# A transformer trunk on one core: the first 512 query channels projected together, row by row

## The chip, the cores and the metric

The kernel runs on 1 core of one Trainium2 chip. The time is that of the device for one execution, in microseconds (us); the runs of the kernel before have a median of 479.36 us (479.05 to 480.07, three runs). Lower is better. The core's engines are TensorE (PE in the profile, with its weight loads as PEld), VectorE (DVE), ScalarE (ACT), GpSimd (POOL) and SyncE (SP), which here issues all loads and stores.

## The reference

One layer of a hybrid decoder: 256 positions, 1024 channels, float32.

```python
def mixer_sublayer(x, w_in, ...):
    qa, ka, va, qd, kd, vd, b_gate, c_gate, hc, gate_logits = jnp.split(x @ w_in, split_points, axis=-1)
    y_moba = moba_attention(heads(qa, 8), heads(ka, 8), heads(va, 8))
    y_conv = b_gate * causal_dwconv(c_gate * hc, w_short_conv)
    y_dil = dilated_mixture(heads(qd, 12), heads(kd, 12), heads(vd, 12))
    gates = jax.nn.sigmoid(gate_logits).reshape(b, s, 3, 1024)
    merged = gates[:, :, 0] * (y_moba @ w_moba_proj) + gates[:, :, 1] * (y_conv @ w_conv_proj) \
        + gates[:, :, 2] * (y_dil @ w_dil_proj)
    return merged @ w_mix_out

def conv_ffn_sublayer(x, w_up, w_ffn_conv, b_ffn_conv, w_down):
    u = causal_dwconv(x @ w_up, w_ffn_conv) + b_ffn_conv
    gate, val = jnp.split(u, 2, axis=-1)
    return (jax.nn.silu(gate) * val) @ w_down

x = layer_norm(DN_ALPHA * x + mixer_sublayer(x, ...), ln1_g, ln1_b)
x = layer_norm(DN_ALPHA * x + conv_ffn_sublayer(x, ...), ln2_g, ln2_b)
```

The change concerns the start alone: x is transposed, and the first columns of `x @ w_in` that are computed are those of the dilated attention, `qd` (768 channels), then `kd` (768) and `vd` (768).

## The kernel before

Products of float32 are made of three products of rounded halves: `split` rounds a tensor to a high part (a cast on ScalarE, line 149) and takes the rest as a low part (a difference on VectorE, line 150), and `mm3` (lines 200 to 202) multiplies high by high, low by high and high by low.

Weights come in blocks of 1 MB (1024 rows by 256 columns), in the order in which `block` and `columns` list them: three blocks of `qd`, three of `kd`, three of `vd`, and so on. `load_next` issues the load of the next block into one of three buffers `raw`, from SyncE's queue (line 124). A block has four pieces of 128 x 512; `prep` splits the next piece, and when the last piece of a block is split, its buffer is free and `load_next` issues another load into it. `ready` holds the split pieces, `used` counts those that are used up, and `prep` goes at most 10 pieces (`LEAD`) ahead of it. The first two blocks are loaded in four parts of 256 KB each, and between those of the first block the four parts of x (line 177).

`transpose_x` turns two of the eight slices of x (128 channels by 256 positions each) on TensorE into a bank of PSUM from the pool `att` (five banks), and splits them into `xTh` and `xTl`. `first_products` then multiplies with one piece of the first block: two slices of x, and two banks of 128 channels each (`o`, from the pool `acc`, which has three banks; the first was used by the warm-up). The other blocks go through `project`: for each half of 128 channels it takes one `acc` bank, multiplies through all eight slices (24 matmuls), and lets `tick` split further pieces and call `consume`, which copies the bank out. For queries and keys a bank is copied out in two halves of 64 partitions, by ScalarE and VectorE in turn (`queries`, lines 239 and 240).

`small_loads` issues five loads of some KB each (the weights of the two convolutions) behind the last block of queries, `rows` loads the two rows of the norm (512 KB each, since they are spread to all partitions), and `small_weights` turns the small loads on TensorE (lines 423 and 425), between the first and the second block of `kd`.

The order of the instructions on each engine is set by a scheduler when the program is built: it goes by the order of the code and takes later work ahead where it holds an engine to be free. On the chip each engine's instructions stand in that fixed order.

Of the kernel before, what the change touches and what calls it, by code (L numbers as in the profile page):

```python
# [14 lines left out]
P = 128  # L15
T = 256
D = 1024
KT = D // P
# [8 lines left out]
DIL_Q, DIL_K, DIL_V = 1536, 2304, 3072  # L27
# [3 lines left out]
RAW = 3  # L31
LEAD = 10
B2 = 61
WARM = 7


@with_exitstack
def trunk(ctx: ExitStack, tc, x, w_in, w_short_conv, w_moba_proj, w_dil_proj, w_conv_proj, w_mix_out,
          ln1_g, ln1_b, w_up, w_ffn_conv, b_ffn_conv, w_down, ln2_g, ln2_b, out):
    nc = tc.nc  # L40
# [12 lines left out]
    def fresh(name):  # L53
        serial[0] += 1
        return f"{name}{serial[0]}"

    def buf(dt=F32, shape=(P, 512)):
        return act.tile(list(shape), dt, tag="b2", name=fresh("b"), bufs=B2)

    def acc(shape=(P, 512)):  # L60
        return ps.tile(list(shape), F32, tag="acc", name=fresh("acc"), bufs=3)

    def att(shape=(P, 512)):
        return ps.tile(list(shape), F32, tag="att", name=fresh("att"), bufs=5)
# [5 lines left out]
    def block(*parts):  # L70

        blocks.append(parts)

    def kview(w, c0, c1, k0=0, k1=None):
        k1 = w.shape[0] // P if k1 is None else k1
        return w[k0 * P:k1 * P, c0:c1].rearrange("(k p) c -> p k c", p=P)

    def columns(base, n):
        for b in range(n):
            c = base + 256 * b  # L80
            block(kview(w_in, c, c + 256))

    columns(DIL_Q, 3)
    columns(DIL_K, 3)
    columns(DIL_V, 3)
    columns(MOBA_V, 2)
# [6 lines left out]
    for d in range(4):  # L93
        for g in range(3):
            columns(GATE + g * D + d * 256, 1)
        c = d * 256
# [11 lines left out]
    loads, pieces, ready = [], [], []  # L108
    used = [0]

    def load_next(between=None):
        i = len(loads)
        if i >= len(blocks):
            return
        r = act.tile([P, 2048], F32, tag="raw", name=fresh("raw"), bufs=RAW)
        at = 0
        for p in blocks[i]:
            k, c = p.shape[1:]
            step = 2 if i < 2 else k
            for k0 in range(0, k, step):  # L120
                if between:
                    between(k0 // step)
                n = step * c
                nc.sync.dma_start(r[:, at:at + n].rearrange("p (k c) -> p k c", c=c), p[:, k0:k0 + step, :])  # L124
                at += n
        loads.append(r)
        pieces.extend((r, c, c + 512 == at) for c in range(0, at, 512))

    def prep(n=1):

        for _ in range(n):
            i = len(ready)
            if i >= min(len(pieces), used[0] + LEAD):
                return
            r, c, last = pieces[i]
            h, l = buf(F32R), buf(F32R)
            split(r[:, c:c + 512], h, l)
            ready.append((h, l))
            if last:
                load_next()  # L140

    def take(n):

        i = used[0]
        assert len(ready) >= i + n, (len(ready), i, n)
        return ready[i:i + n]

    def split(src, h, l):
        nc.scalar.copy(h, src)  # L149
        nc.vector.tensor_sub(l, src, h.bitcast(F32))  # L150
# [4 lines left out]
    def tick(n, consume=None, ahead=1):  # L155


        used[0] += n
        while late:
            late.pop(0)()  # L160
        prep(n + ahead)
        if consume:
            consume()
        if side:
            side.pop(0)()
# [4 lines left out]
    wps = acc()  # L170
    for i in range(WARM):
        nc.tensor.matmul(wps, warm[:, :P], warm, start=True, stop=True)


    xs = act.tile([P, 2, D], F32, tag="xs", name="xs", bufs=2)
    xv = x.rearrange("(t p) c -> p t c", p=P)
    load_next(lambda c: nc.sync.dma_start(xs[:, :, c * 256:c * 256 + 256], xv[:, :, c * 256:c * 256 + 256]))  # L177
    for i in range(1, RAW):
        load_next()

    ident = const.tile([P, P], F32, name="ident")
    diff = const.tile([P, P], I32, name="diff")
# [3 lines left out]
    xTh = act.tile([P, KT, T], F32R, tag="xTh", name="xTh")  # L186
    xTl = act.tile([P, KT, T], F32R, tag="xTl", name="xTl")

    def transpose_x(k2):
        k = 2 * k2  # L190
        p = att((P, 2, T))
        for a in range(2):
            for t in range(2):
                nc.tensor.transpose(p[:, a, t * P:(t + 1) * P], xs[:, t, (k + a) * P:(k + a + 1) * P], ident)  # L194
        split(p, xTh[:, k:k + 2, :], xTl[:, k:k + 2, :])


    def mm3(o, ah, al, bh, bl, first, last):
# [10 lines left out]
    def project(consume, xh=xTh, xl=xTl, ahead=1):  # L209

        w = take(4)
        for c in range(2):
            o = acc((P, T))
            for k in range(KT):
                mm3(o, *cut(w, k, c * P, c * P + P), xh[:, k, :], xl[:, k, :], k == 0, k == KT - 1)
            tick(2, lambda: consume(c, o), ahead)
# [16 lines left out]
    def queries(store):  # L233

        def consume(c, o):
            q = buf(F32R, (P, 2, T))
            for a in range(2):
                s, n = HALF[a], HALF[1 - a]
                nc.scalar.copy(q[s, a, :], o[s, :])
                nc.vector.tensor_sub(q[n, a, :], o[s, :], q.bitcast(F32)[s, a, :])  # L240
            store.append(q)
        return consume
# [185 lines left out]


    dq, dk, dv = [[], [], []], [[], [], []], []  # L430
    o = [acc((P, T)) for _ in range(2)]

    def first_products(k2):
        w = ready[k2]
        for xt, i in ((xTh, 0), (xTl, 0), (xTh, 1)):
            for k in (2 * k2, 2 * k2 + 1):
                for c in range(2):
                    s = (k % 2) * 256 + c * P
                    nc.tensor.matmul(o[c], w[i][:, s:s + P], xt[:, k, :], start=k + i == 0 and xt is xTh,  # L439
                                     stop=k == KT - 1 and i == 1)  # L440

    for k2 in range(KT // 2):
        transpose_x(k2)
        prep()
        if k2:
            first_products(k2 - 1)
    first_products(KT // 2 - 1)
    q = queries(dq[0])
    for c in range(2):
        tick(2, lambda: q(c, o[c]), 1)  # L450
    for g in range(1, 3):
        project(queries(dq[g]), ahead=0)
    small_loads()
    gB, bB = rows(ln1_g, "gB"), rows(ln1_b, "bB")
# [5 lines left out]
    p, q = (dilated(c, dq, dk, dv, [t[:, c, :] for t in yd]) for c in range(2))  # L460
# [6 lines left out]
    for b in range(2):  # L467
# [21 lines left out]
        p, q = (moba(c, mq, mk, mv[b], [t[:, c, :] for t in ym]) for c in range(2))  # L489
# [15 lines left out]
    for d in range(4):  # L505
        gs = []
        for g in range(3):
            s = buf(F32, (P, 2, T))
# [5 lines left out]
        w = take(5)  # L514
        for c in range(2):
            for g, k0, n, ys in ((2, 0, 2, [yd]), (1, 2, 4, ycT), (0, 6, 4, ymT)):
                o = acc((P, T))
# [81 lines left out]
    w = take(4)  # L599
# [15 lines left out]
    def between():  # L615
        passed.append(prep(1))
        if len(passed) == 2:
            turn_x1(0, 0)
            turn_x1(0, 1)
# [29 lines left out]
    w = take(8)  # L649
    u = []  # L650
    for t in range(2):
        o = acc()
        s = slice(t * P, (t + 1) * P)
# [23 lines left out]
    for j in range(2, NJ, 2):  # L677
# [3 lines left out]
        while 2 < j < NJ - 2 and pend:  # L681
            w = take(4)
# [49 lines left out]
```

## Time and profile before

| | |
|---|---|
| profiled execution | 479.29 us |
| its span, from first to last instruction | 477.5 us |
| median of the runs | 479.36 us |
| TensorE busy | 466.5 us, 98% of the span |
| VectorE busy | 360.3 us, 75% |
| ScalarE busy | 271.0 us, 57% |
| mean granted clock of TensorE | 0.991 |
| bytes moved | 83.51 MB, mean 175 GB/s |

The span is what lies between the first and the last instruction; the rest of an execution's time lies around it. Matmuls are pipelined: the profile gives one as 283 ns, while they start 0.12 us apart. The idle time of an engine matters only where the chain of waits goes through it.

### The profile page before, as it was taken

To read this page: it belongs to the slowest core of one execution; us is meant where nothing else is said; L and a number is where in the kernel's file an instruction comes from. 1 tells how busy PE (TensorE), PEld (TensorE's weight loads), DVE (VectorE), ACT (ScalarE), POOL (GpSimd) and SP (SyncE) were. 2 spreads that over 40 slices of the span, in tenths; PEclk is the share of its full clock that TensorE was granted. 3 is DMA by queue.
4 is the path that set the end of the run, shared out by engine and by line. 5 is a ranking of instruction groups with operands and counts; after the bars stand their busy time and mean duration, and the time that the engine had idled before them with its cause. 6 is when DMAs were issued, how large, how long until landed. Compare 5 with 4: busy or idle time off the path is not lost.

```text
span 477.5 us, 9121 instructions
## 1 busy us (share of the span) xinstructions
PE 466.5 (98%) x3582; PEld 450.6 (94%) x3582; DVE 360.3 (75%) x775; ACT 271.0 (57%) x579; POOL 10.4 (2%) x29
## 2 busy tenths in 40 slices
PE   7999999999999999999999999999999999999993
PEld 4999999999999999999999899999999999999983
DVE  6788996778989757484748866997867676786966
ACT  4767774737668645454545316866555565564710
POOL 1100000010100000000000000000000000000000
PEclk8999999999999999999999999999999999999997
DMA  8986555254451745656465914657465545637002
GB/s 265 359 253 189 178 177 177 89 176 131 136 161 41 231 144 182 195 165 211 153 220 200 311 49 151 243 175 265 127 227 176 178 177 188 221 122 244 21 2 88
DMA packets 69502, 83.51 MB, mean 175 GB/s; under 512 B 1688, under 2 KB 64852, under 8 KB 69460
## 3 DMA queue, kind: packets, MB, share of 16 engines
q1 hardware_dynamic: 69460, 82.94, 53.3%
q8 instruction: 28, 0.46, 0.4%
q14 instruction: 14, 0.11, 0.1%
HBM read 81.89 MB, written 1.05 MB: 174 GB/s over the span
## 4 chain that ended last, share of the span: by engine, by line
PE 97%; DMA 1%; DVE 1%; SPq 0%; ACT 0%; issue 0%; DVEq 0%
PE acc L200 24%; PE acc L202 24%; PE acc L201 24%; PE att L201 7%; PE att L200 7%; PE att L202 7%; PE att L266 2%; PE acc L439 1%; PE att L287 1%; DMA xs<-in_x_dram 1%; PE att L194 0%; DVE r L551 0%; SPq L124 0%; SPq L177 0%; PE acc L594 0%
## 5 line engine op out<-in xcount | busy, mean ns | idle before, releaser
L150 DVE TENSOR_TENSOR b<-raw,b 128x512 fp32r<-128x512 f32 x300 | 196.1, 687 | 38.0 <-ACT b L149 35.6
L149 ACT CAST b<-raw 128x512 fp32r<-128x512 f32 x300 | 169.3, 620 | 6.2 <-DMA raw<-in_w_in_dram 2.9
L200 PE MATMUL acc<-xTh,b 128*128 128x256 f32 x432 | 122.9, 284 | 0.0
L201 PE MATMUL acc<-xTl,b 128*128 128x256 f32 x432 | 122.2, 283 | 0.0
L202 PE MATMUL acc<-xTh,b 128*128 128x256 f32 x432 | 122.2, 283 | 0.0
L200 PE MATMUL acc<-x1Th,b 128*128 128x256 f32 x320 | 90.9, 284 | 0.0
L202 PE MATMUL acc<-x1Th,b 128*128 128x256 f32 x320 | 90.6, 283 | 0.0
L201 PE MATMUL acc<-x1Tl,b 128*128 128x256 f32 x320 | 90.5, 283 | 0.0
L200 PEld LDWEIGHTS acc<-xTh,b 128*128 128x128 f32 x432 | 82.8, 192 | 0.2
L201 PEld LDWEIGHTS acc<-xTl,b 128*128 128x128 f32 x432 | 82.9, 192 | 0.0
L202 PEld LDWEIGHTS acc<-xTh,b 128*128 128x128 f32 x432 | 82.9, 192 | 0.0
L201 PEld LDWEIGHTS acc<-x1Tl,b 128*128 128x128 f32 x320 | 61.4, 192 | 0.1
L200 PEld LDWEIGHTS acc<-x1Th,b 128*128 128x128 f32 x320 | 61.4, 192 | 0.1
L202 PEld LDWEIGHTS acc<-x1Th,b 128*128 128x128 f32 x320 | 61.4, 192 | 0.0
L629 DVE SCALAR_TENSOR_TENSOR b<-acc,fconv,b 128x255 f32<-128x255 f32 x80 | 38.5, 481 | 30.2 <-ACT b L627 29.2
L200 PE MATMUL att<-b,b 128*128 128x512 f32 (+1 forms) x170 | 58.9, 347 | 0.0
L201 PE MATMUL att<-b,b 128*128 128x512 f32 (+1 forms) x170 | 58.9, 347 | 0.0
L202 PE MATMUL att<-b,b 128*128 128x512 f32 (+1 forms) x170 | 58.7, 345 | 0.0
L149 ACT CAST b<-b 128x256 fp32r<-128x256 f32 x34 | 13.8, 408 | 46.8 <-DVE b L525 23.4
L627 ACT ACTIVATE b<-acc,fconv 128x256 f32<-128x256 f32 x40 | 22.6, 565 | 28.6 <-PE acc L202 28.6
L200 PEld LDWEIGHTS att<-b,b 128*128 128x128 f32 x170 | 32.2, 189 | 4.0
L202 PEld LDWEIGHTS att<-b,b 128*128 128x128 f32 x170 | 32.1, 189 | 4.0
(108 smaller groups left out, 625.0 us busy)
## 6 DMA issues: line engine op xcount, KB each, us to landing
raw<-in_w_in_dram SPq DMA_DIRECT2D x31, 1024.0 KB, 5.7
raw<-in_w_up_dram SPq DMA_DIRECT2D x22, 1024.0 KB, 5.4
raw<-in_w_down_dram SPq DMA_DIRECT2D x11, 1024.0 KB, 5.0
raw<-in_w_mix_out_dram SPq DMA_DIRECT2D x4, 1024.0 KB, 5.3
raw<-in_w_in_dram SPq DMA_DIRECT2D x8, 256.0 KB, 6.2
raw<-in_w_conv_proj_dram SPq DMA_DIRECT2D x4, 512.0 KB, 3.5
raw<-in_w_moba_proj_dram SPq DMA_DIRECT2D x4, 512.0 KB, 4.6
xs<-in_x_dram SPq DMA_DIRECT2D x4, 256.0 KB, 3.6
```

What stands on the lines that cost most here:

```text
L149: nc.scalar.copy(h, src)
L150: nc.vector.tensor_sub(l, src, h.bitcast(F32))
L200: nc.tensor.matmul(o, ah, bh, start=first, stop=False)
L201: nc.tensor.matmul(o, ah, bl, start=False, stop=False)
L202: nc.tensor.matmul(o, al, bh, start=False, stop=last)
L266: nc.tensor.matmul(o, qt, k[i][:, a, :], start=i == 0, stop=i == 1)
L287: nc.tensor.transpose(p[:, i, :], b, ident)
L439: nc.tensor.matmul(o[c], w[i][:, s:s + P], xt[:, k, :], start=k + i == 0 and xt is xTh, stop=k == KT - 1 and i == 1)
L627: nc.scalar.activation(v, o, AF.Identity, bias=w[3], scale=w[0])
L629: nc.vector.scalar_tensor_tensor(v[:, j:], o[:, :T - j], w[j], v[:, j:], op0=OP.mult, op1=OP.add)
```

## The change

The first two blocks, so far columns of 256, become one set of 512 columns, cut by rows: a piece is now one slice of 128 rows by 512 columns, which serves one slice of x and four banks of 128 channels. Two of these banks come from `acc`, two from `att`. x comes in five parts (slices 0, 1, 2 and 3, 4 and 5, 6 and 7), each behind a weight row or two. The order of transposes and products on TensorE is forced by `issue_after`. `used` counts up with every piece, and behind the fifth to eighth piece two further pieces each are split, which are those of the third block and of the fourth (the first of `kd`). The four banks are copied out behind that. The third block is loaded in four parts. The warm-up has one matmul less.

```diff
-WARM = 7
+WARM = 6
...
-    columns(DIL_Q, 3)
+    for k in (0, 4):
+        block(kview(w_in, DIL_Q, DIL_Q + 512, k, k + 4))
+    columns(DIL_Q + 512, 1)
...
-            step = 2 if i < 2 else k
+            step = 1 if i < 2 else 2 if i == 2 else k
...
-    load_next(lambda c: nc.sync.dma_start(xs[:, :, c * 256:c * 256 + 256], xv[:, :, c * 256:c * 256 + 256]))
-    for i in range(1, RAW):
-        load_next()
+    X_PARTS = {0: 1, 1: 2, 2: 4, 4: 6, 6: 8}
+    def load_x(k):
+        if k in X_PARTS:
+            c = slice(k * P, X_PARTS[k] * P)
+            nc.sync.dma_start(xs[:, :, c], xv[:, :, c])
+    for i in range(RAW):
+        load_next(load_x if i < 2 else None)
...
-    o = [acc((P, T)) for _ in range(2)]
+    o = [(acc if c < 2 else att)((P, T)) for c in range(4)]
+    def first_products(k):
+        w = ready[k]
         for xt, i in ((xTh, 0), (xTl, 0), (xTh, 1)):
+            for c in range(4):
+                last = nc.tensor.matmul(o[c], w[i][:, c * P:c * P + P], xt[:, k, :], start=k + i == 0 and xt is xTh,
+                                        stop=k == KT - 1 and i == 1)
+        used[0] += 1
+        return last
+    def behind(last, f, *args):
+        if last is None:
+            return f(*args)
+        with tc.issue_after(last.ins):
+            return f(*args)
+    last = None
+    for step in (0, 1, 'p', 2, 'p', 4, 'p', 'p', 6, 'p', 'p', 'p', 'p'):
+        if step == 'p':
+            last = behind(last, first_products, used[0])
+            prep(2 if used[0] > 4 else 0)
+        else:
+            last = behind(last, transpose_x, step, X_PARTS[step])
+            prep(X_PARTS[step] - step)
+    for g in range(2):
+        q = queries(dq[g])
+        for c in range(2):
+            q(c, o[2 * g + c])
+            prep()
+    for g in range(2, 3):
         project(queries(dq[g]), ahead=0)
```

Where it moves instructions, in three places. First, TensorE right behind the warm-up (`xs` is x, `att` of line 194 or 201 a bank for transposes, `b` a split piece). Before:

```order
L194 MATMUL att_116<-ident,xs 128x128 x4
L194 MATMUL att_127<-ident,xs 128x128 x4
L194 MATMUL att_150<-ident,xs 128x128 x4
L439 MATMUL acc_114<-xTh,b_123 128x256
L439 MATMUL acc_115<-xTh,b_123 128x256
L439 MATMUL acc_114<-xTh,b_123 128x256
L439 MATMUL acc_115<-xTh,b_123 128x256
L194 MATMUL att_173<-ident,xs 128x128 x2
```

And after:

```order
L201 MATMUL att_121<-ident,xs 128x128 x2
L201 MATMUL att_130<-ident,xs 128x128 x2
L446 MATMUL acc_117<-xTh,b_126 128x256
L446 MATMUL acc_118<-xTh,b_126 128x256
L446 MATMUL att_119<-xTh,b_126 128x256
L446 MATMUL att_120<-xTh,b_126 128x256
L446 MATMUL acc_117<-xTl,b_126 128x256
L446 MATMUL acc_118<-xTl,b_126 128x256
L446 MATMUL att_119<-xTl,b_126 128x256
L446 MATMUL att_120<-xTl,b_126 128x256
```

The first product stood behind the transposes of six slices of x and now stands behind those of two.

Second, ScalarE where the first banks are copied out (`acc_114` before, `acc_117` after; `raw` is a loaded block: `raw_84` the second, `raw_89` the third, `raw_166` and `raw_234` the first two of `kd`). Before:

```order
L149 CAST xTh<-att_173 128x512
L149 CAST b_214<-raw_84 128x512
L149 CAST b_218<-raw_84 128x512
L239 CAST b_222<-acc_114 64x256
L149 CAST b_227<-raw_84 128x512
L239 CAST b_222<-acc_114 64x256
L149 CAST b_233<-raw_89 128x512
```

And after:

```order
L151 CAST b_268<-raw_89 128x512
L151 CAST xTh<-att_219 128x512
L151 CAST b_272<-raw_89 128x512
L151 CAST b_290<-raw_166 128x512
L151 CAST b_294<-raw_166 128x512
L151 CAST b_310<-raw_166 128x512
L151 CAST b_314<-raw_166 128x512
L247 CAST b_320<-acc_117 64x256
L151 CAST b_325<-raw_234 128x512
L247 CAST b_320<-acc_117 64x256
L247 CAST b_329<-acc_118 64x256
```

The copy of the first bank stood between the pieces of the second block, and now stands behind all of the first block of `kd`, its second half behind a piece of the second. VectorE follows in the same order; there, from the second half of that bank on (`acc_348` is the bank of the third block's first half, `raw_276` the third block of `kd`), after the change:

```order
L248 TENSOR_TENSOR b_320<-acc_117,b_320 64x256
L248 TENSOR_TENSOR b_329<-acc_118,b_329 64x256
L152 TENSOR_TENSOR b_335<-raw_234,b_334 128x512
L248 TENSOR_TENSOR b_338<-att_119,b_338 64x256
L248 TENSOR_TENSOR b_329<-acc_118,b_329 64x256
L248 TENSOR_TENSOR b_343<-att_120,b_343 64x256
L248 TENSOR_TENSOR b_338<-att_119,b_338 64x256
L152 TENSOR_TENSOR b_374<-raw_234,b_373 128x512
L248 TENSOR_TENSOR b_343<-att_120,b_343 64x256
L152 TENSOR_TENSOR b_378<-raw_234,b_377 128x512
L248 TENSOR_TENSOR b_383<-acc_348,b_383 64x256
L152 TENSOR_TENSOR b_414<-raw_276,b_413 128x512
```

One more piece of `raw_276` and the second half of `acc_348` come next. Before, the copies of two banks never stood together like this: two pieces and two halves took turns.

Third, SyncE's queue from the first row of the norm (`gB`) on. Before:

```order
L409 DMA gB_407<-in_ln_g_dram 128x1024
L124 DMA raw_184<-in_w_in_dram 128x8x256
L409 DMA bB_409<-in_ln_b_dram 128x1024
L124 DMA raw_231<-in_w_in_dram 128x8x256
L124 DMA raw_279<-in_w_in_dram 128x8x256
L124 DMA raw_357<-in_w_in_dram 128x8x256
L415 DMA b_112<-in_w_short_conv_dram 12x128
```

And after:

```order
L417 DMA gB_431<-in_ln_g_dram 128x1024
L126 DMA raw_166<-in_w_in_dram 128x8x256
L126 DMA raw_234<-in_w_in_dram 128x8x256
L126 DMA raw_276<-in_w_in_dram 128x8x256
L126 DMA raw_318<-in_w_in_dram 128x8x256
L417 DMA bB_433<-in_ln_b_dram 128x1024
L126 DMA raw_381<-in_w_in_dram 128x8x256
L423 DMA b_115<-in_w_short_conv_dram 12x128
```

The second row of the norm went from between the first two blocks of `kd` to behind the first block of `vd` (`raw_318`), and the small loads from behind the first block of `vd` (`raw_357` before) to behind the second (`raw_381`).

More of the change, by code (lines that the diff above doesn't have):

```diff
@@ L118, in load_next @@
             k, c = p.shape[1:]
-            step = 2 if i < 2 else k
+            step = 1 if i < 2 else 2 if i == 2 else k
             for k0 in range(0, k, step):
                 if between:
-                    between(k0 // step)
+                    between(i * 4 + k0)
                 n = step * c
@@ L187, in trunk, with transpose_x @@
     xTl = act.tile([P, KT, T], F32R, tag="xTl", name="xTl")
[L189 to L192, printed above, removed]
+    def transpose_x(k, k1):
+        p = att((P, k1 - k, T))
+        for a in range(k1 - k):
             for t in range(2):
-                nc.tensor.transpose(p[:, a, t * P:(t + 1) * P], xs[:, t, (k + a) * P:(k + a + 1) * P], ident)
-        split(p, xTh[:, k:k + 2, :], xTl[:, k:k + 2, :])
+                i = nc.tensor.transpose(p[:, a, t * P:(t + 1) * P], xs[:, t, (k + a) * P:(k + a + 1) * P], ident)
+        split(p, xTh[:, k:k1, :], xTl[:, k:k1, :])
+        return i
     def mm3(o, ah, al, bh, bl, first, last):
@@ L430, in trunk @@
     dq, dk, dv = [[], [], []], [[], [], []], []
-    o = [acc((P, T)) for _ in range(2)]
-    def first_products(k2):
-        w = ready[k2]
+    o = [(acc if c < 2 else att)((P, T)) for c in range(4)]
+    def first_products(k):
+        w = ready[k]
         for xt, i in ((xTh, 0), (xTl, 0), (xTh, 1)):
[L436 to L451, printed above, removed]
+            for c in range(4):
[22 more added lines that the diff above has]
+    for g in range(2, 3):
         project(queries(dq[g]), ahead=0)
```

## The prediction

> **What bounds the kernel now.** I read the page first, then the chain of waits, then the first 36 us in order of time, since the diff touches nothing behind them.
>
> ```profile
> span 477.5 us, 9121 instructions
> PE 466.5 (98%) x3582; PEld 450.6 (94%) x3582; DVE 360.3 (75%) x775; ACT 271.0 (57%) x579; POOL 10.4 (2%) x29
> PE 97%; DMA 1%; DVE 1%; SPq 0%; ACT 0%; issue 0%; DVEq 0%
> ```
>
> TensorE carries 97% of the chain, so only time in which it stands still or runs at half clock can be won, or lost. The view by stretches (columns as its second line names them) shows where that is.
>
> ```profile
> core 0: us, PE busy (x) PEld busy (x) DVE busy (x) ACT busy (x) POOL busy (x), PEclk, DMA share, GB/s
> 2.00:13.10 11.10, 8.82 (x45) 6.81 (x44) 6.71 (x14) 4.55 (x9) 1.14 (x4) 0.85 1.00 318
> 13.10:20.40 7.30, 7.30 (x63) 7.30 (x62) 5.49 (x10) 5.75 (x12) 0.62 (x2) 1.00 1.08 368
> 4.49:7.90 3.41, 1.13 (x9) 0.66 (x7) 2.30 (x4) 2.21 (x4) 0.00 (x0) 1.00 0.95 302
> 7.90:11.31 3.41, 3.41 (x16) 3.41 (x17) 1.95 (x4) 2.15 (x4) 0.00 (x0) 0.50 1.05 355
> 11.31:16.10 4.79, 4.79 (x43) 4.79 (x41) 2.80 (x5) 1.81 (x4) 0.62 (x2) 1.00 1.09 361
> 16.10:33.60 17.50, 17.50 (x146) 17.28 (x144) 15.69 (x30) 13.76 (x30) 1.23 (x4) 1.00 0.91 285
> ```
>
> TensorE does little up to 7.90 us (1.13 of the last 3.41), then has half the clock for 3.41 us, and is full from 11.31 on. Two other things are full: the DMA engines up to 20.40 (share 1.0 and more), and VectorE, busy 15.69 of 17.50 us from 16.10 on. A change that starts TensorE sooner runs into these two. The fixed points in time:
>
> ```profile
> 7.88 1.11 PE L194 MATMUL att<-ident,xs 128*128 128x128 f32 x4 [1.64 <-DMA xs<-in_x_dram]
> 8.64 1.20 PE L439 MATMUL acc<-xTh,b 128*128 128x256 f32 x4
> 13.43 0.59 ACT L149 CAST xTh<-att 128x512 fp32r<-128x512 f32 x1 [1.94 <-PE att L194]
> 13.91 1.14 ACT L149 CAST b<-raw 128x512 fp32r<-128x512 f32 x2
> 16.10 0.28 PE L200 MATMUL acc<-xTh,b 128*128 128x256 f32 x1
> 21.95 0.35 PE L200 MATMUL acc<-xTh,b 128*128 128x256 f32 x1
> 33.62 0.23 PE L423 MATMUL att<-ident,b 12*128 12x12 f32 x1
> ```
>
> The third transpose waits for its x until 7.88 and the first product stands behind it at 8.64. The second block starts at 16.10, the third at 21.95: 5.85/48 = 0.12 us a matmul. So half the third block is done at 21.95 + 24 x 0.12 = 24.8, the second half of the first key block starts at 21.95 + 72 x 0.12 = 30.6, and the transposes of the small weights at 33.62. These are the marks for the sum.
>
> **Prices.** Durations of one, and of pairs in a row:
>
> ```profile
> L150 DVE TENSOR_TENSOR b<-raw,b 128x512 fp32r<-128x512 f32 x40 | 26.3, 684 | 2.4 <-ACT b L149 2.0
> L149 ACT CAST b<-raw 128x512 fp32r<-128x512 f32 x41 | 24.0, 620 | 3.1 <-DMA raw<-in_w_in_dram 2.9
> L240 DVE TENSOR_TENSOR b<-acc,b 64x256 fp32r<-64x256 f32 x12 | 5.1, 423 | 1.4 <-ACT b L239 1.1
> L239 ACT CAST b<-acc 64x256 fp32r<-64x256 f32 x12 | 4.4, 368 | 3.9 <-DVE b L240 2.3 <-PE acc L439 1.1 <-PE acc L202 0.4
> L150 DVE TENSOR_TENSOR xTl<-att,xTh 128x512 fp32r<-128x512 f32 x4 | 2.8, 690 | 3.4 <-ACT xTh L149 3.3
> L149 ACT CAST xTh<-att 128x512 fp32r<-128x512 f32 x4 | 2.3, 585 | 3.9 <-PE att L194 3.9
> ...
> 22.29 1.30 DVE L150 TENSOR_TENSOR b<-raw,b 128x512 fp32r<-128x512 f32 x2
> 23.62 0.88 DVE L240 TENSOR_TENSOR b<-acc,b 64x256 fp32r<-64x256 f32 x2
> ```
>
> A weight piece costs VectorE 0.65 us, a half of a query bank 0.44, ScalarE 0.57 (1.14 for two) and 0.37.
>
> The landings, from the queue's rows (issue, and us to landing):
>
> ```profile
> 5.81 0.81 SPq L124 DMA_DIRECT2D raw<-in_w_in_dram  x1
> raw<-in_w_in_dram SPq DMA_DIRECT2D x2, 256.0 KB, 6.5
> 25.85 0.37 SPq L124 DMA_DIRECT2D raw<-in_w_in_dram  x1
> raw<-in_w_in_dram SPq DMA_DIRECT2D x1, 1024.0 KB, 6.1
> raw<-in_w_in_dram SPq DMA_DIRECT2D x1, 1024.0 KB, 5.6
> raw<-in_w_down_dram SPq DMA_DIRECT2D x11, 1024.0 KB, 5.0
> raw<-in_w_mix_out_dram SPq DMA_DIRECT2D x4, 1024.0 KB, 5.3
> ```
>
> The load issued at 5.81 is the 11th of 256 KB in the queue (four of x, four and three of the two blocks) and landed at 5.81 + 6.5 = 12.3. From there the engines move 0.361 to 0.368 MB a us, so 256 KB take 0.72 us. The change keeps the bytes and their order: x and two blocks, third block, one norm row, first key block. So the third block's third piece (unit 15) lands at 12.3 + 4 x 0.72 = 15.2, and the first key block (unit 22) at 12.3 + 11 x 0.72 = 20.2 us. Call that L. The second key block is no longer behind the other norm row and lands 1.05 MB/0.368 = 2.85 us later, at 23.05.
>
> **Front.** x's first 128 KB and the first weight row are 1.5 units instead of 2, so they land before 4.8; a cast of 0.62 and one of half an xTh make the first product start near 5.5 instead of 8.64. That gain isn't kept whole, because ScalarE takes its work in the order written: at 13.43 it has stood 1.94 us waiting for TensorE, while a piece that the queue had brought before 12.3 was cast only at 13.91. In the new order the cast of x's rows 6 and 7 stands behind the third block's third piece: 15.2, two casts (0.62 and 0.59) to 16.4; on VectorE that piece's difference to 16.5 and xTl to 17.2. Then the last 8 matmuls of row 6, 12 of row 7 and 24 of the third block take 44 x 0.12 = 5.3: first half done at 22.5 instead of 24.8. **Gain standing there: 2.3 us.** The dropped warm-up matmul and the extra cast of the split x lie before the first landings and cost nothing; if the clock were at half from 4.5 to 7.9 for that reason, the waits for landings behind it cover it.
>
> **First wait.** The second half of the third block needs an `acc` bank. There are three: the first half took the warm-up's, and the other two hold the first 512 channels until they are copied out. In the new order this copy stands on ScalarE and VectorE behind all four pieces of the first key block, and its second half behind the first piece of the second key block. From L = 20.2: cast to 20.85, four differences (2 x 1.30) to 23.45, first half of the bank to 23.9; the next block lands at 23.05, its cast ends at 23.7, its difference at 24.55, the bank's second half at 25.0. TensorE stands from 22.5 to 25.0, and the gain is gone: 25.0 against 24.8, **+0.2**.
>
> **Second wait.** The second half of the first key block needs the bank of the third block's first half. VectorE has 13 more operations until that is copied, eight of 0.44 and five of 0.65, all without a gap: 6.8 us, to 31.8. TensorE would be there at 25.0 + 48 x 0.12 = 30.8 and was there at 30.6: **+1.2**.
>
> **Third wait.** The small weights are issued behind the load of the second value block, and that one needs VectorE's ninth operation of those 13 (six of 0.44, three of 0.65): 25.0 + 4.6 = 29.6. A load of 1 MB lands 5.6 to 6.1 us after its issue: 35.2 to 35.7, I take 35.4, and the small ones just behind, 35.5. TensorE gets to their transposes at 31.8 + 2.9 = 34.7 and was there at 33.62: **+1.9**. Before, they stood behind the load issued at 25.85 (landing 32.0), in time. Nothing later is reordered in a way that TensorE waits for: the splits stand further ahead of it than before.
>
> **Sum.** The profiled execution took 479.29 us (span 477.5 and 1.8 around it), the runs' median 479.36, so both give the same: 479.3 + 1.9 = **481.2 us**.
>
> **Unknown prices.** L: nothing in the trace has rows of 2 KB (the new weight rows) or 512 bytes (x's first two parts). Loads with 4 KB rows land after 5.0 to 5.3 us where those with 1 KB take 5.6: over 2 MB up to 1.2 us sooner; x's small parts at most as dear as 256 KB, 2 x 0.36 = 0.7 later. L between 19.0 and 20.9; I take 20.2, since most loads are like the quoted ones. All three waits move with L one for one. The small weights: right behind the 1 MB load (35.5), or, if they pass it, no wait at all, which leaves +1.2. By the Trainium skill (DMA: Bandwidth & Descriptors, Specifications) runs of 512 bytes still go at full rate, by which the 0.7 would fall away; no row here shows it.
>
> **Rivals.** *Faster: the loads come early.* If 2 KB rows bring the first key block at 17.3 instead of 20.2, the waits fall to -1.0 in all: 478.3 us or less; below L = 18.3 it decides. That would ask for 5.77 MB by 17.3 us, some 0.38 MB a us from 2 us on, against 318 in 2 to 13.1 above: 0.08. *No change:* the small weights land in time and L is half a us sooner, +0.7, 480.0; or L near 18.5: 0.16. *A clock drop on top:* in 4.49 to 7.90 TensorE was busy 1.13 of 3.41 us, and the next 3.41 us had clock 0.50. The pause of 2.5 us in the first wait can leave as little. One such stretch costs 14 matmuls, 1.7 us, and hides in the second and third wait (1.0 and 0.8); two in a row cost 3.4, TensorE reaches the small weights at 37.1: 482.8. Chance 0.06. The Trainium skill (TensorE: Matmul & The Clock Gate, HAM oscillation) has the clock fall only after pauses above about 3.4 us, and (Part 4) transposes not counted as work; the row agrees, as what ran there was transposes. By that rule the pause costs nothing, by the row it may. The forecast itself, all three waits with L from 19.3 to 20.9, has 0.70.
>
> **Numbers.** A measurement of this kernel tells about 0.2%, 1.0 us, from no change. Slower by more: 0.70 and 0.06, 0.76; within: 0.16; faster: 0.08. The range leaves out the faster case and little above 482.8, the two-stretch drop: 479.5 to 482.8.
>
> **What would show it.** Right: first product near 5.5; TensorE idle some 2.5 us before the third block's second half, the releaser VectorE at the bank's difference; a pause of about 1 us two projections later, one before the small transposes; then none, and the clock at 1.0. Wrong: the first key block's casts well before 20 us, or the bank's copy ahead of them.

## The result: slower, and by more than forecast

The changed kernel takes 483.96 us (median of 4 runs, 483.61 to 485.75), the kernel before 479.21 us beside it (4 runs, 478.78 to 480.07): a ratio of 1.0104, 95% interval 1.0075 to 1.0134. It is slower by 4.75 us, where 1.9 was forecast. The profiled execution took 484.22 us. Its page and its table of TensorE's waits:

```profile
span 482.1 us, 9131 instructions
PE 91%; DMA 5%; DVE 2%; ACT 0%; issue 0%; SPq 0%; DVEq 0%
```

```profile
engine line waited for: us in total, times, longest us
PE acc L208 <- DVE b L248: 2.6, 1, 2.6
PE acc L174 <- DVE warm L171: 1.2, 1, 1.2
PE att L201 <- DMA xs<-in_x_dram: 1.0, 1, 1.0
PE att L431 <- DMA b<-in_w_short_conv_dram: 0.4, 1, 0.4
```

TensorE's share of the chain fell from 97% to 91%; what came in is a load (DMA, 5%) and VectorE. The wait of 2.6 us is new (that of 1.2 us is the start of the warm-up). Where it lies shows the view in order of time (start, duration, engine and line, what ended the idle time before it):

```profile
5.81 0.80 PE L446 MATMUL acc<-xTh,b 128*128 128x256 f32 x2
...
20.98 0.28 PE L208 MATMUL acc<-xTh,b 128*128 128x256 f32 x1
21.41 2.19 ACT L151 CAST b<-raw 128x512 fp32r<-128x512 f32 x4 [3.38 <-DMA raw<-in_w_in_dram]
22.06 2.50 DVE L152 TENSOR_TENSOR b<-raw,b 128x512 fp32r<-128x512 f32 x4 [3.03 <-ACT b L151]
24.59 0.42 DVE L248 TENSOR_TENSOR b<-acc,b 64x256 fp32r<-64x256 f32 x1
24.67 0.62 ACT L151 CAST b<-raw 128x512 fp32r<-128x512 f32 x1 [0.81 <-DMA raw<-in_w_in_dram]
25.32 0.69 DVE L152 TENSOR_TENSOR b<-raw,b 128x512 fp32r<-128x512 f32 x1 [0.31 <-ACT b L151]
26.04 0.88 DVE L248 TENSOR_TENSOR b<-acc,b 64x256 fp32r<-64x256 f32 x2
26.62 0.36 PE L208 MATMUL acc<-xTh,b 128*128 128x256 f32 x1 [2.60 <-DVE b L248]
31.36 0.37 SPq L126 DMA_DIRECT2D raw<-in_w_in_dram  x1
37.33 0.23 PE L431 MATMUL att<-ident,b 12*128 12x12 f32 x1 [0.37 <-DMA b<-in_w_short_conv_dram]
...
38.04 0.26 PE L433 MATMUL att<-ident,b 44*128 44x44 f32 x1
38.23 0.39 PE L208 MATMUL acc<-xTh,b 128*128 128x256 f32 x1
...
40.49 0.25 PE L433 MATMUL att<-ident,b 44*128 44x44 f32 x1
40.67 0.39 PE L210 MATMUL acc<-xTh,b 128*128 128x256 f32 x1
```

Read from the top: the first product starts at 5.81 us instead of 8.64, the third block at 20.98 instead of 21.95. ScalarE then stands 3.38 us for the first key block, which lands at 21.4; its four pieces and one of the next block go ahead of the second half of the bank's copy on both engines, and TensorE, out of banks, stands from 23.9 to 26.62 (the kernel before went on at 24.8 without a wait). At the small transposes it is 3.7 us behind (37.33 against 33.62), and 1.1 us more are lost just there: the four transposes at line 433 stand one by one among the matmuls of the next projection, where before they came in a row:

```profile
33.78 0.44 PE L425 MATMUL att<-ident,b 44*128 44x44 f32 x4
```

From there on the lag stays within 0.03 us of 4.84 us up to the last products: 3.7 + 1.1.

The stretches of both kernels (columns as in the prediction), first of the kernel after, then of the one before:

```profile
core 0: us, PE busy (x) PEld busy (x) DVE busy (x) ACT busy (x) POOL busy (x), PEclk, DMA share, GB/s
5.81:10.45 4.64, 4.64 (x22) 4.64 (x22) 2.28 (x5) 2.08 (x4) 0.61 (x2) 1.00 1.02 343
10.45:20.98 10.53, 10.53 (x88) 10.47 (x88) 7.74 (x13) 6.26 (x12) 1.23 (x4) 1.00 1.08 363
19.00:22.00 3.00, 3.00 (x27) 3.00 (x27) 0.03 (x1) 0.59 (x2) 0.61 (x2) 1.00 1.10 350
24.10:27.52 3.42, 0.90 (x7) 0.93 (x8) 2.98 (x6) 2.68 (x7) 0.00 (x0) 1.00 0.89 260
27.52:30.93 3.41, 3.41 (x18) 3.41 (x17) 3.21 (x8) 2.93 (x8) 0.61 (x2) 0.50 0.98 353
```

```profile
19.00:22.00 3.00, 3.00 (x27) 2.89 (x25) 2.88 (x6) 2.84 (x7) 0.61 (x2) 1.00 1.06 372
```

Three things are to be seen. From 5.81 to 10.45 TensorE does 22 instructions in 4.64 us, 0.21 each, later 0.12: the first products run at half speed, though the column says 1.00 (the first record of the granted clock in this execution is at 10.45, and what stands before it is not known). From 27.52 to 30.93 the clock is 0.50, behind the pause. And from 19 to 22 us, where both engines that split and copy were full in the kernel before (2.88 and 2.84 of 3 us), VectorE now does next to nothing (0.03) and ScalarE 0.59: every piece that has landed is split, the banks are finished together only at 20.98, and the next block lands at 21.4. After that VectorE is busy nearly without a gap.

### The profile page after: what moved, and what is told of

The parts are those of the page before. It is cut to its first block, busy times and chain, and to the rows that moved or that the text cites. A ratio compares the mean times of both kernels' runs of the same rounds, so it can differ in the third digit from the quotient of the medians.

```text
span 482.1 us, 9131 instructions
## 1 busy us (share of the span) xinstructions
PE 469.7 (97%) x3581; PEld 453.2 (94%) x3581; DVE 360.4 (75%) x776; ACT 271.3 (56%) x580; POOL 10.3 (2%) x29
## 4 chain that ended last, share of the span: by engine, by line
PE 91%; DMA 5%; DVE 2%; ACT 0%; issue 0%; SPq 0%; DVEq 0%
PE acc L210 22%; PE acc L208 22%; PE acc L209 22%; PE att L209 6%; PE att L208 6%; PE att L210 6%; DMA raw<-in_w_in_dram 4%; PE att L274 2%; PE att L295 1%; DMA b<-in_w_short_conv_dram 1%; DVE b L152 1%; DVE b L248 1%; ACT b L151 0%; DVE r L570 0%; PE acc L613 0%
## 5 line engine op out<-in xcount | busy, mean ns | idle before, releaser
L208 PE MATMUL acc<-xTh,b 128*128 128x256 f32 x416 | 119.2, 287 | 2.6 <-DVE b L248 2.6
L209 PE MATMUL acc<-xTl,b 128*128 128x256 f32 x416 | 118.7, 285 | 0.0
L210 PE MATMUL acc<-xTh,b 128*128 128x256 f32 x416 | 118.5, 285 | 0.0
L208 PEld LDWEIGHTS acc<-xTh,b 128*128 128x128 f32 x416 | 80.5, 193 | 2.8 <-issue 2.8
L210 PEld LDWEIGHTS acc<-xTh,b 128*128 128x128 f32 x416 | 80.6, 194 | 0.1
L209 PEld LDWEIGHTS acc<-xTl,b 128*128 128x128 f32 x416 | 80.5, 194 | 0.1
```

The costliest lines, as they stand in the source:

```text
L208: nc.tensor.matmul(o, ah, bh, start=first, stop=False)
L209: nc.tensor.matmul(o, ah, bl, start=False, stop=False)
L210: nc.tensor.matmul(o, al, bh, start=False, stop=last)
```

## The experiments

Each was timed beside runs of the kernel before; ratios are to those. "Late" small transposes are those of the small weights, moved by empty places in the list `side`.

| run | what differs from the changed kernel | us, median | ratio to before (95%) |
|---|---|---|---|
| e1 | first key block's pieces between the copies | 482.75 | 1.0062 (1.0047 to 1.0077) |
| e2 | small transposes late | 482.26 | 1.0051 (1.0036 to 1.0066) |
| e3 | third block's second half in the other pool | 487.75 | 1.0162 (1.0146 to 1.0178) |
| e4 | e2 and e3 | 483.67 | 1.0086 (1.0067 to 1.0104) |
| e5 | e4, first key block's differences on GpSimd | 484.08 | 1.0096 (1.0080 to 1.0111) |
| e6 | x in four parts | 483.73 | 1.0087 (1.0071 to 1.0103) |
| e7 | e4, no pieces among the copies | 480.62 | 1.0033 (1.0018 to 1.0047) |
| e8 | e7, x in four parts | 479.16 | 0.9997 (0.9983 to 1.0010) |
| e9 | e4, eight differences left out | 481.54 | 1.0044 (1.0025 to 1.0062) |
| e10 | copies first, then first key block, x in four parts, late | 479.02 | 0.9987 (0.9974 to 1.0001) |
| e11 | e10, one key copy on ScalarE | 479.11 | 0.9987 (0.9975 to 1.0000) |
| e12 | e11, nine warm-ups | 478.92 | 0.9984 (0.9969 to 0.9998) |
| e13 | e4, copies of the first 512 channels left out | 479.02 | 1.0001 (0.9987 to 1.0014) |
| e14 | e12 and e3 | 478.20 | 0.9979 (0.9967 to 0.9991) |
| e15 | nine warm-ups | 483.93 | 1.0099 (1.0071 to 1.0127) |

The first theory was that of the prediction, called the queue theory in the expectations: what stands ahead of the bank copies in the two engines' order, and the small loads behind it. Its rivals: the clock (pause and half clock are the price by themselves), and the landings (the bytes come late, the order doesn't matter).

### One wait at a time

**e1.**

```diff
-            prep(2 if used[0] > 4 else 0)
+            prep(2 if 4 < used[0] <= 6 else 0)
```

> One part undone: only the third block is split ahead; the first key block's four pieces come between the copies of the four banks instead of ahead of them. Queue theory (the loss comes from what ScalarE and VectorE have in front of the copies, and from the small loads behind it): TensorE runs from the third block's first half (done near 23.9 us) into the second without a pause, no half clock after it, first key block done near 32.6 us instead of 37.0, at most half a us of waiting at the small transposes and some 0.6 us for their interleaving: 479.1 us (478.3 to 480.2). Clock theory (the pause and the half clock stretch are the price, 1.8 + 1.5 us, and nothing else): 484.0 - 3.3 = 480.7 us. Landing theory (late landings of the rows are the price, the order of the copies is not): 483 us or more.

482.75 us, which fits none of the theories: above the first two, just under the third. TensorE's waits, in order of time:

```profile
24.55 0.36 PE L208 MATMUL acc<-xTh,b 128*128 128x256 f32 x1 [0.95 <-DVE b L248]
32.99 0.36 PE L208 MATMUL acc<-xTh,b 128*128 128x256 f32 x1 [2.47 <-DVE b L248]
```

The first wait shrinks from 2.60 to 0.95, and another of 2.47, for the bank of the third block's first half, takes its place. Moving the pieces changes where TensorE waits, and little of how long. The first key block landed at 22.58 us in this execution, 1.2 later than in the changed kernel's, which is in these waits too.

**e2 and e3**, each alone.

```diff
-    side += [lambda: None, small_weights]
+    side += [lambda: None] * 4 + [small_weights]
```

> The transposes of the small weights are done three half projections later and nothing else is moved, no transfer and no split. Queue theory: pause and half clock stay as they are, the wait of 0.4 us at these transposes and 1.1 us of their interleaving go: 482.5 us (482.0 to 483.0). Clock theory: interleaving costs nothing by itself, 483.6 to 484.0 us.

```diff
-            o = acc((P, T))
+            o = pools[c]((P, T))
...
-        project(queries(dq[g]), ahead=0)
+        project(queries(dq[g]), ahead=0, pools=(acc, att))
```

> The third block's second half is given a bank of the other pool, and nothing else is changed. Queue theory: TensorE runs on at 23.9 us without a pause and without the half clock, is done with the first key block near 32.6 us, and then stands for the small loads, which land near 37.3 us as before: 484 us, up to 485.7 if the pause of 4.7 us there is followed by half clock. Clock theory: 484.0 - 3.3 = 480.7 us.

e2 came out as the queue theory says: third wait and scattered transposes together are worth 1.7 us by the medians, 2.5 by the ratios. Its trace shows more (waits, then two stretches):

```profile
26.32 0.36 PE L208 MATMUL acc<-xTh,b 128*128 128x256 f32 x1 [2.64 <-DVE b L248]
33.43 0.36 PE L208 MATMUL acc<-xTh,b 128*128 128x256 f32 x1 [1.13 <-DVE b L248]
```

```profile
21.69:25.11 3.42, 2.00 (x17) 1.79 (x15) 3.00 (x6) 2.85 (x7) 0.00 (x0) 1.00 1.09 346
25.11:28.52 3.41, 2.20 (x18) 2.23 (x19) 3.22 (x7) 3.06 (x8) 0.42 (x2) 1.00 0.87 265
```

The same pause is followed by no half clock here, and the second wait of the prediction, which the changed kernel's trace lacked, stands at 33.43. In that trace the half clock had covered it: the same matmul started at 33.92 there. So the half clock cost at most 0.5 us in the changed kernel's profiled execution, and the clock theory's 1.5 is refuted there. The other executions agree: the one with the highest granted clock (0.997) took 483.69 us, two with 0.992 took 483.61 and 484.22 (the fourth, at 0.990, took 485.75).

e3 does not bring the clock theory's gain either: the first wait is gone, and the kernel is slower by 3 to 4 us (ratios, medians), not faster by 3.3.

```profile
PE att L431 <- DMA b<-in_w_short_conv_dram: 4.6, 1, 4.6
```

```profile
32.96:36.38 3.42, 0.00 (x0) 0.00 (x0) 2.67 (x7) 2.42 (x6) 0.00 (x0) 1.00 0.98 318
36.38:39.79 3.41, 2.58 (x10) 2.02 (x10) 3.20 (x7) 2.20 (x6) 0.00 (x0) 0.50 0.69 189
```

TensorE comes to the small transposes earlier and waits 4.6 us for the same late loads; then the clock is at half for three stretches, 10.2 us (36.38 to 46.62), with nothing behind it to hide in. The wait moved as forecast; the price of the clock behind it was larger, 484 to 485.7 were expected and 487.75 came. So half clock by itself is not the loss, but it costs time where no wait follows that would have been there anyway.

**e4**, both edits:

> Both: the other bank for the third block's second half, and the small transposes three half projections later. Queue theory: neither pause is left but about 1 us before the second key block, whose bank is copied near 33.6 us; 479.2 - 0.6 = 478.6 us (478.0 to 479.6), that is 5.4 us less than the changed kernel, though the two edits alone give 0 and 1.5. Clock theory: 480.7 us, as with the other bank alone.

483.67 us, and 481.41 in the profiled execution, against 478.6. In that execution no half clock follows the waits (granted clock 0.998); the other three, at 0.992 to 0.994, took 483.47 to 484.61, so half clock is a likely part of the median. With two waits out of the way a third appeared that was not in the sum:

```profile
PE acc L208 <- DVE b L266: 2.3, 1, 2.3
PE acc L208 <- DVE b L248: 0.8, 1, 0.8
```

The bank of the first key half is copied out as late as the others were. The queue theory names each wait rightly and does not say why they come back one bank later each time. Since both engines were found idle from 19 to 22 us, the next theory was VectorE's: its list starts late and paces the stretch.

### What paces the stretch

**e5.**

```diff
-            split(r[:, c:c + 512], h, l)
+            split(r[:, c:c + 512], h, l, nc.gpsimd if 12 <= i < 16 else nc.vector)
```

> The kernel with the other bank and the late small transposes, and the four differences of the first key block's pieces done by GpSimd instead of VectorE, so that VectorE has 2.5 us less to do just after 22 us. VectorE theory (VectorE paces this stretch: it stands 3 us from 19 to 22, and its backlog then holds every bank up; the last query difference comes at 34.5 us instead of 29.95, and TensorE lags by as much): the waits of 0.8 us before 33.5 and 2.3 us near 37 go, 481.4 - 2.6 = 478.8 us, as long as GpSimd's four differences end before 28.9 us. Landing theory (the weights come late, VectorE only follows them): the weights land as before, 481.4 us or more.

484.08 us; no verdict, for a reason the trace shows:

```profile
23.77 5.47 POOL L152 TENSOR_TENSOR b<-raw,b 128x512 fp32r<-128x512 f32 x4 [22.71 <-ACT b L151]
```

```profile
26.69 1.42 DVE L152 TENSOR_TENSOR b<-raw,b 128x512 fp32r<-128x512 f32 x1 [0.72 <-ACT b L151]
```

GpSimd takes 1.37 us for a difference that takes VectorE 0.65, VectorE's own takes 1.42 beside it, and the first key block was split from 23.1 us on in this execution, 1.7 us later than in the changed kernel.

**e6 to e8.**

```diff
-    X_PARTS = {0: 1, 1: 2, 2: 4, 4: 6, 6: 8}
+    X_PARTS = {0: 2, 2: 4, 4: 6, 6: 8}
...
-    for step in (0, 1, 'p', 2, 'p', 4, 'p', 'p', 6, 'p', 'p', 'p', 'p'):
+    for step in (0, 'p', 2, 'p', 4, 'p', 'p', 6, 'p', 'p', 'p', 'p'):
```

> The changed kernel, with x loaded and transposed in four parts of 256 KB as in the kernel before, everything else as changed. If the small parts of x (512 bytes a row) made the landings late: third block's last piece lands near 16.1 instead of 17.1 us, first key block near 20.4 instead of 21.4, all waits kept but 1.0 us earlier: 483.0 us. If the weight rows or something else did: 484.0 us, landings unchanged.

483.73 us, no gain that can be told. By the completion events of the loads the third block's last piece landed at 15.80 us instead of 17.11, as expected if x's small parts delay it; but the first key block landed at 21.64, not 20.4: fifteen of the sixteen parts in which a load completes were there by 19.90, the last one 1.7 us later. So the small parts of x did cost 1.3 us of landing, and the last part of one load hid it. The other traces bear out the first half: the third block's last piece lands at 16.7 to 17.2 us in the ten executions with x in five parts, at 15.5 to 16.2 in the six with four.

e7 is e4 with this edit; e8 is e7 with x in four parts.

```diff
             q(c, o[2 * g + c])
-            prep()
```

> The kernel with the other bank and the late small transposes, and in addition no pieces of the second key block split between the copies of the four banks (they come two half projections later, when TensorE needs them). VectorE theory: the bank of the third block's first half is free near 31.3 instead of 33.5 us, before TensorE needs it at 32.6, and the next key bank near 35.7 (needed at 35.5): no wait over 0.3 us after 24 us, 478.3 us (477.8 to 479.5). Landing theory: 481.4 us, since the same bytes land at the same times.

> As the run with no pieces ahead, with x in four parts of 256 KB. VectorE theory, with the landings 1.0 us earlier: 478.3 - 1.0 = 477.3 us, faster than the kernel before by 2 us. If x's parts make no difference: 478.3 us. Landing theory: 480.4 us.

480.62 and 479.16 us: each step that moves the lists forward brings something, 3.1 us for four pieces out of the copies' way (by the medians; 1.4 between the profiled executions, 481.41 and 479.99, of which neither has half clock in this stretch), 1.5 for x. The one wait left behind 24 us, of e7 and of e8:

```profile
37.12 0.36 PE L208 MATMUL acc<-xTh,b 128*128 128x256 f32 x1 [1.37 <-DVE b L266]
```

```profile
36.15 0.36 PE L208 MATMUL acc<-xTh,b 128*128 128x256 f32 x1 [0.39 <-DVE b L266]
```

The first key block landed at 21.50 and 20.52, so the wait follows the landing one for one: the landing sets when the lists begin. Both kernels fell short of their forecasts by about 2 us: the wait for the first key half's bank was put at 0.3 at most, and the front, taken as 1 us ahead, was 0.75 (the third block starts at 21.20 us in both, at 21.95 in the kernel before).

**e9** leaves VectorE's part of the copies out. Here and in e13 the small transposes are also tied to each other, behind the last matmul ahead of them, which keeps them in a row; in e4's trace they stood in a row already.

```diff
-                nc.vector.tensor_sub(q[n, a, :], o[s, :], q.bitcast(F32)[s, a, :])
+                if low:
+                    nc.vector.tensor_sub(q[n, a, :], o[s, :], q.bitcast(F32)[s, a, :])
+                else:
+                    nc.gpsimd.memset(q.bitcast(F32)[n, a, :], 0.0)
```

> The kernel with the other bank and the late small transposes, with eight differences of 0.42 us left out on VectorE: the low halves of the first 512 channels' queries are set to zero by GpSimd instead (so that part of the result is left out). The run on GpSimd's differences could not tell, since they slowed VectorE and the first key block landed 1.7 us later there. VectorE theory: its list is 3.5 us shorter, no wait over 0.3 us between 24 and 45 us, TensorE keeps the 1.0 us that it is ahead at 23.9 us: 478.4 us (477.8 to 479.2), all runs alike since no pause lowers the clock. Landing theory: the key weights land as before, waits of 0.8 and 2.3 us stay, 481.4 to 484 us.

481.54 us. The VectorE theory falls: with 3.5 us less to do, VectorE stands for ScalarE, and TensorE's wait is as long as in e4 (rows of VectorE and of TensorE; the first key block landed at 21.88 us here, 0.7 later than in e4, which is a part of it but not the whole):

```profile
29.15 1.30 DVE L152 TENSOR_TENSOR b<-raw,b 128x512 fp32r<-128x512 f32 x2 [1.47 <-ACT b L151]
...
38.19 0.36 PE L210 MATMUL acc<-xTh,b 128*128 128x256 f32 x1 [2.26 <-DVE b L271]
```

Which engine is the full one changes with the edit (columns as above, first e4, then e9):

```profile
22.00:34.00 12.00, 11.16 (x93) 10.98 (x92) 11.08 (x21) 8.89 (x21) 1.23 (x4) 1.00 0.84 269
22.00:34.00 12.00, 11.70 (x98) 11.53 (x98) 8.16 (x14) 10.27 (x23) 1.23 (x4) 1.00 0.89 283
```

In e4 VectorE is busy 11.08 of 12 us and ScalarE stands for it; in e9 ScalarE is busy 10.27 and VectorE, with 8.16, stands for ScalarE.

**e13** leaves out both engines' parts.

```diff
+                if not real:
+                    for h in (s, n):
+                        nc.gpsimd.memset(q.bitcast(F32)[h, a, :], 0.0)
+                    continue
                 nc.scalar.copy(q[s, a, :], o[s, :])
```

> The kernel with the other bank and the late small transposes, with the copies of the first 512 channels left out on both ScalarE and VectorE (their queries are set to zero by GpSimd, so that part of the result is left out). The run that left out only VectorE's half had VectorE standing 1.5 us for ScalarE, so VectorE's list alone does not pace the stretch. Joint theory (the lists of ScalarE and VectorE together, which stand from 19 to 21.4 us and then run behind): each list is about 3 us shorter, the bank of the first key half is free near 33.5 us, before TensorE needs it at 35.5; no wait over 0.3 us from 24 to 45 us: 478.4 us (477.8 to 479.3). Landing theory (the pieces behind the landings of the key blocks hold the banks whatever else is in the lists): the waits of 0.8 and 2.3 us stay, 481.4 us or more.

479.02 us, and all of TensorE's waits are these, none after 9 us:

```profile
PE att L201 <- DMA xs<-in_x_dram: 1.4, 2, 1.1
PE acc L174 <- DVE warm L171: 1.2, 1, 1.2
```

The key blocks landed within 0.3 us of where they did in e4 (20.95, 23.99 and 26.88 us; 21.20, 24.26 and 27.13 there), and both of e4's waits are gone. The landing theory, by which the landings hold the banks whatever else is in the lists, falls; what paces is the two lists together, which follow each other piece by piece. No run left out ScalarE's part alone; that it would not do is argued from e4, where ScalarE stands for VectorE.

### Where the front's gain went, and a better version

**e15** is the changed kernel with more warm-up.

```diff
-WARM = 6
+WARM = 9
```

> The changed kernel with nine warm-up matmuls instead of six, nothing else. In the changed kernel the first products ran at half clock from 5.8 to 10.4 us (0.21 us apart), and the third block's first half was done at 23.9 us. Joint theory: with full clock from about 6 us that half is done 1 to 2 us earlier, and the pause before the second half grows by as much, since the bank's copy stands behind the landing of the first key block: 484.0 us, the gain at the front is lost there. Clock theory of the front: the 1.5 to 2 us come through to the end, 482.2 us.

483.93 us, and the gain of the front is lost in the wait, which grows from 2.60 to 2.96:

```profile
26.55 0.36 PE L208 MATMUL acc<-xTh,b 128*128 128x256 f32 x1 [2.96 <-DVE b L248]
33.66 0.36 PE L208 MATMUL acc<-xTh,b 128*128 128x256 f32 x1 [1.13 <-DVE b L248]
```

The gain itself is smaller than expected. The granted clock is recorded as full from 4.87 us on in this execution (as early as in several with six warm-up matmuls, so the edit need not be the reason), and still the third block's first half is done only 0.4 us earlier. The limit is another: TensorE's product with the low part of x's rows 6 and 7 starts just when VectorE has made that part, in the changed kernel and in e15:

```profile
17.75 0.68 DVE L152 TENSOR_TENSOR xTl<-att,xTh 128x512 fp32r<-128x512 f32 x1
18.49 0.50 PE L446 MATMUL acc<-xTl,b 128*128 128x256 f32 x2
```

```profile
17.32 0.68 DVE L152 TENSOR_TENSOR xTl<-att,xTh 128x512 fp32r<-128x512 f32 x1
18.06 0.50 PE L446 MATMUL acc<-xTl,b 128*128 128x256 f32 x2
```

That part stands behind the third block's third piece, which landed at 16.39 and at 15.98 us.

**e10, e11, e12 and e14** put the order right: third block split ahead, the four copies, then the first key block's pieces, x in four parts, small transposes late and in a row (each behind the last matmul ahead of it).

```diff
-            prep(2 if used[0] > 4 else 0)
+            prep(2 if 4 < used[0] <= 6 else 0)
...
             q(c, o[2 * g + c])
-            prep()
+    prep(4)
     for g in range(2, 3):
```

> Candidate: x in four parts; only the third block split ahead; then the copies of the four banks, then the first key block's pieces; second key block's pieces where TensorE needs them; small transposes late and in a row; no bank of the other pool. VectorE theory: the copies start near 20.7 us in VectorE's idle time instead of after the first key block's landing, its list is about 1 us ahead of the run with no pieces ahead and x in four parts, whose wait of 0.4 us goes: 478.6 us (478.0 to 479.3), and neither pause nor half clock after 24 us. If VectorE's start isn't what counts: 479.2 us as there.

e11 adds the next edit, e12 the nine warm-up matmuls of e15, e14 the bank of e3.

```diff
-                if a:
+                if a or any(store is d for d in dk):
                     nc.scalar.copy(k[n, a, :], o[s, :])
```

> The candidate, with one copy of 0.42 us in each half of the three key blocks done by ScalarE (0.37) instead of VectorE. VectorE theory: where the candidate has no wait for VectorE left, 478.6 us as it; where it has one, that much less. If ScalarE becomes the bound (its casts and copies go from 2.25 to 2.6 us in the 2.9 us of a half): 479 us or more, with waits that end at ScalarE.

> As the run with keys on ScalarE, with nine warm-up matmuls instead of six, which end near 4.9 us. Clock theory of the front: the first products run at half clock until about 10 us in some runs (0.21 us apart) and until about 5 in others; with TensorE busy from 2.4 to 5 us full clock is there at 6 us in all, worth up to 1.6 us less the landings' wait: 478.0 us. Landing theory of the front (the last piece of the third block sets its end): no change, 478.6 us.

> The candidate with nine warm-up matmuls and keys on ScalarE, and the third block's second half in a bank of the other pool: its one wait, 1.06 us near 30 us for the bank of the third block's first half, goes. Joint theory: the wait moves two half projections back, where the bank is free: 478.9 - 0.9 = 478.0 us, faster than the kernel before by 1.3 us. Rival: the lists are as late there, the wait comes back one bank later: 478.9 us.

e10 to e12 are level with the kernel before or barely faster, and no better among themselves: the same wait stands in each (e10: 1.06 us at 30.58, for the bank of the third block's first half), and neither ScalarE's help nor the early clock lies on the path. With the other bank (e14) it goes and does not come back, and 478.20 us is faster than before by 0.21% (0.09 to 0.33). Its stretch from 19 to 22 us, and VectorE's first copy there:

```profile
19.00:22.00 3.00, 3.00 (x27) 3.00 (x27) 1.39 (x4) 1.86 (x7) 0.61 (x2) 1.00 1.10 347
```

```profile
20.49 0.75 DVE L250 TENSOR_TENSOR b<-acc,b 64x256 fp32r<-64x256 f32 x2 [2.83 <-ACT b L249]
```

The copies run while the first key block, at 21.12 us in this execution, is still on its way.

## Why the prediction was right and wrong

**The direction and the path were right.** The first product came at 5.81 us (forecast 5.5); the second half of the third block waits for a bank whose copy stands behind five pieces, its releaser VectorE; the second wait is there (1.13 us in e2, forecast 1.0), unless a half clock covers it, which the prediction had too; the small transposes wait behind the load issued last.

**The term that was mis-sized is L, the landing of the first key block.** It was taken as 20.2 us, with 20.9 as the late end; it was 21.39, and the next block came at 24.65 instead of 23.05. That puts the first wait's end at 26.62 instead of 25.0 and the load ahead of the small weights at 31.36 instead of 29.6, 1.8 us later, and its landing took the time forecast. "All three waits move with L one for one" held: the lag at the small transposes is 3.7 us, 1.9 + 1.8. The step "x's small parts at most as dear as 256 KB, 2 x 0.36" failed: e6's third block landed 1.3 us earlier without them, its last piece at 15.80, where the prediction's count puts that piece (12.3 + 5 x 0.72 = 15.9); so the weight rows of 2 KB, the other unknown of L, changed nothing that can be seen. The late end should also have been wider for another reason, which no row of the kernel before showed: over the traces here the first key block lands between 20.0 (e10) and 23.0 us (e5), since one of its sixteen parts can be 1.7 to 1.9 us behind the rest. By the Trainium skill (DMA: Bandwidth & Descriptors, Specifications) runs of 512 bytes go at full rate; e6 against the changed kernel does not bear that out for these parts, but it changes their size too, so the runs' length alone was not tried.

**A term was missing:** the four small transposes among the matmuls. The prediction counted a wait before them and priced their place at nothing. From 33.62 against 37.33 to the constant 4.84 they cost 1.1 us. 1.9 + 1.8 + 1.1 = 4.8, measured 4.75.

**The front's gain was over-counted by the same term:** 2.3 us at the third block's first half, measured 1.0 (23.9 against 24.8). The limit that the prediction named is the right one, the third block's third piece and the splits behind it. It took the piece to land at 15.2 and the splits to end at 17.2; the piece landed at 16.39, and they ended at 18.43. TensorE ran without a gap from 5.81 on, the first 4.6 us at 0.21 an instruction, and came to this point just when it was free to go on: the half clock at the start was covered, as the prediction said, and e15, without it, gained only what its piece landed earlier. The error cost nothing in the time, since the first wait took the gain whatever its size.

**The faster rival** needed the first key block below 18.3 us; no trace here has it before 20.0. **The rival of the clock** came once, as one stretch, and hid as the prediction said; in e3, where nothing was behind it to hide in, 10.2 us of it came, and the time was 2 us above the upper forecast. What the sum did not see at all is what makes the waits come back: both copying engines are idle from 19 to 22 us, in a stretch where they had been full, so that every bank in their lists is late and removing one wait (e1, e3, e4) shows the next. e13 shows that the length of the two lists is what counts; that filling the idle stretch cures it is seen in e14, where no wait is left, only together with its other edits.

Open: why a load's last part is late in some executions, what the length of x's runs alone costs, and what half clock adds to the medians of e4 and e9, whose executions differ in it.

## What to carry to other kernels

Count the work that the helpers (here the two engines that split and copy) can do in each stretch, not only the place of one copy in their order: a change that makes several banks ready at one moment takes the copies out of an idle stretch and puts them into a full one. Where engines work in order, don't put work that waits for a load ahead of a copy that frees a bank; and when a wait that is removed comes back one buffer later, look for the late list and not for the next wait. Look in the order of instructions also for small ones that a scheduler has strewn among the matmuls: here 0.3 us each.

## What the runs showed of the hardware

- The clock does not go by the length of the pause alone. The recorded changes of the clock in one execution lie whole multiples of 3.41 us apart (changed kernel: 10.45, 27.52 and 30.93 us), so the time can be cut into stretches of 3.41 us from them. Stretches with TensorE busy 0.90 (changed kernel), 1.13 (kernel before, with transposes only) and 0.00 us (e3) were followed by half clock; e2's pause was as long (2.64 us) and e15's longer (2.96), but they fell across two stretches, busy 2.00 and 2.20 us in e2 and 1.66 and 2.21 in e15, and none followed. The border lies between 1.50 us (e5, followed by half clock) and 1.63 (e4, not). The Trainium skill (TensorE: Matmul & The Clock Gate, HAM oscillation) asks for no gaps above about 3.4 us; 2.60 us was enough here, so by these runs the rule is too mild. Its free-running window of 3.4 us (same page, on the clock gate) agrees with the stretches.
- A difference of 128x512 took GpSimd 1.37 us, and VectorE's own, beside it, took 1.42 instead of 0.69 (one case, e5; a copy out of a bank beside it kept its 0.42).
- One load completes in sixteen parts that can lie 1.7 to 1.9 us apart at the end (e6: 19.90 and 21.64 us; e5: 21.12 and 23.04); whoever waits for the load waits for the last.
